# Hybrid diffusion block: the input projections of layer 0 start on rows that are scaled but not shifted, and layer 1 starts three such projections instead of five

## The chip, the cores and the metric

One NeuronCore of a Trainium2 chip runs the whole program. The metric is the device time of one execution in microseconds (us), the median of several runs; lower is better. Engines are named as in the profile: PE (TensorE matmuls) and PEld (its weight loads), DVE (VectorE), ACT (ScalarE), POOL (GpSimd), SP (SyncE, which issues the DMAs).

## The reference, cut to what matters

Two layers over 384 columns: 128 context tokens (stream 0) and 256 latent tokens (stream 1), each with its own modulation vector, model width 1024. What matters here is the head of each layer:

```
mod = silu(cond) @ w_ada + b_ada              # one vector per stream
sh1, sc1, g1, sh2, sc2, g2 = split(mod, 6)
h   = rmsnorm(x, norm1_g) * (1 + sc1) + sh1
parts = split(h @ w_in, ...)                  # inputs of three mixers and of their gates
```

The mixers (windowed attention A, latent attention B, a gated delta rule C with a 3-tap convolution in front), their gated sum, an output projection and a squared-ReLU MLP follow.

## The kernel before, in words

Data lie transposed, features on the 128 partitions and the T = 384 tokens along the free axis, so the model width is 8 blocks `k`. Every float32 product is made of float32r halves: `split` (L145 to L147) makes a high part on ACT (L146, `whi`) and the rest on DVE (L147, `wlo`), and `mm3` (L149 to L152) makes three matmuls per `k`. A *projection tile* is 128 outputs: 8 blocks, 24 matmuls, into one PSUM bank. Banks come from pools: `pg` (three banks, tag `g`), `po` (one, `o`), `pc` (two, `c`), `pf` (a pair, `f`, taken by `twin`). A tile framework fixes each engine's order of instructions beforehand from the order of the program and its priorities; every engine then runs its own list in order.

**Layer 0** has the function `lead` (L352 to L414), because its modulation has to be computed from `w_ada` first. It takes `w_ada` in three parts, `PARTS`: four blocks `k` of scale and shift together (eight DMAs of 512 KB), then two and two (sixteen DMAs of 256 KB). For each part, PE multiplies it with the condition (`c<-mraw,cs`, L155, 32 output columns, four matmuls per DMA), DVE transposes the result (L400), adds the bias (L402) and forms the gain `gp` (L404). `modulated` (L216 to L229) then makes the finished `h` of those blocks as `hh` and `hl`: DVE L223 (x times gain times the row factor `rb`), ACT L225 (plus shift, high part), DVE L226 (the rest). Four projection tiles, `w_small` (48 outputs: the decoupled key and the gates of mixer C) and three conv keys of mixer C, run along as far as `h` goes (`advance`). Their banks are two `g` and more; the first is read by ACT into `kab`, the others by the convolution `conv_silu` (ACT L648, DVE L651, L653, ACT L657, DVE L658).

**Layer 1** has its modulation early, but needs the row factor `rb`. So `scaled` (L231 to L244) makes `x` times gain without `rb`, with the shift in two extra columns T and T+1, and five projection tiles (L482 to L490) run on that: three `g` banks and the pair `f`. Meanwhile `modulated` makes the finished `h` for the rest. `normalised` (L546 to L555) later turns such a bank into the finished projection: DVE copies the shift's columns to `eb` (L550) and multiplies by `rb` (`rbs`, L551), ACT adds `eb` (L553).

After the head both layers transpose `kab` (L595), run the chain of the gates on DVE (`z`, `lp`, `gdec`, L597 to L638), and go on with the other tiles of `w_in` through `project` (one `g` bank each): keys and values of mixer A first (`kA`, with the rotation `rope` on DVE: L250 to L253).

Of the kernel before, what the change touches and what calls it, by code (L numbers as in the profile page):

```python
# [18 lines left out]
P = 128  # L19
# [8 lines left out]
B_SCALE = 96.0 ** -0.5  # L28
STREAMS = ((0, slice(0, 128)), (1, slice(128, 384)))

PARTS = ((4, 2), (2, 1), (2, 1))

ADV = (2, 1, 3, 1, 0, 1, 0, 1, 2, 1, 2, 3)

# [10 lines left out]
def trunk(ctx: ExitStack, tc: tile.TileContext, A, O):  # L45
# [4 lines left out]
    def mk(pool, shape, tag, dt=F32, bufs=None):  # L50
        count[0] += 1
        return pool.tile(list(shape), dt, name=f"{tag}_{count[0]}", tag=tag, bufs=bufs)
# [161 lines left out]
    def hidden():  # L214
        return mk(hp, [P, T + 2], "hh", F32R, bufs=KT), mk(hp, [P, T + 2], "hl", F32R, bufs=KT)

    def modulated(rb, gp, sh, sh0, ks=range(KT)):
        his, los = [], []
        for k in ks:
            t = mk(sp, [P, T], "tmp")  # L220
            hi, lo = hidden()
            for s, c in STREAMS:
                V.scalar_tensor_tensor(out=t[:, c], in0=x[k][:, c], scalar=gp[:, k, s:s + 1], in1=rb[:, c],  # L223
                                       op0=ALU.mult, op1=ALU.mult)
                S.activation(hi[:, c], t[:, c], AF.Identity, bias=sh[:, sh0 + k, s:s + 1], scale=1.0)  # L225
                V.scalar_tensor_tensor(out=lo[:, c], in0=t[:, c], scalar=sh[:, sh0 + k, s:s + 1],  # L226
                                       in1=hi[:, c].bitcast(F32), op0=ALU.add, op1=ALU.subtract)
            his.append(hi)
            los.append(lo)  # L229
        return his, los  # L230

    def scaled(gp, sh, sh0):

        his, los = [], []
        for k in range(KT):
            hi, lo = hidden()
            for s, c in STREAMS:
                S.activation(hi[:, c], x[k][:, c], AF.Copy, scale=gp[:, k, s:s + 1])
                V.scalar_tensor_tensor(out=lo[:, c], in0=x[k][:, c], scalar=gp[:, k, s:s + 1],  # L239
                                       in1=hi[:, c].bitcast(F32), op0=ALU.mult, op1=ALU.subtract)  # L240
            split(sh[:, sh0 + k, :], hi[:, T:], lo[:, T:])
            his.append(hi)
            los.append(lo)
        return his, los  # L244
# [105 lines left out]

    early = []

    def lead():
        es = ExitStack()
        lp = area(es, "lead", "right")
        pl = prm[0]
        rb = mk(lp, [P, T], "rb")
        S.copy(rb, rstd_rows(squares(x), 1.0 / DM))
        mod0 = mods[0, 0] = mk(sp, [P, 16, 2], "mod0")
        m0 = mod0.rearrange("p (s b) i -> p s b i", s=2)  # L360
        gp1 = mk(sp, [P, KT, 2], "gp1")
        srcs = [A["w_small"][0]] + [A["w_in"][0, 11 + i] for i in range(4)]
        tiles, at, hh, hl, pair = [], [], [], [], []

        def load():
            src = srcs.pop(0)
            n = src.shape[1]
            raw = mk(wp, [P, 1024], "raw", bufs=3)
            nc.sync.dma_start(raw[:, :n], src)
            hi, lo = mk(lp, [P, 1024], "lhi", F32R, bufs=5), mk(lp, [P, 1024], "llo", F32R, bufs=5)  # L370
            split(raw[:, :n], hi[:, :n], lo[:, :n])
            if len(tiles) == 3:
                pair[:] = twin()
            ps = mk(pg, [P, 512], "g") if len(tiles) < 3 else pair[len(tiles) - 3]
            tiles.append([w[:, :n].rearrange("p (k c) -> p k c", k=KT) for w in (hi, lo)])
            early.append(ps[:n // KT, :T])
            at.append(0)

        def advance(k1):
            for i, (wh, wl) in enumerate(tiles):  # L380
                for k in range(at[i], k1):
                    mm3(early[i], wh[:, k, :], wl[:, k, :], hh[k][:, :T], hl[k][:, :T], k == 0, k == KT - 1)
                at[i] = k1

        b0 = 0
        for nb, nw in PARTS:
            n, b1 = 2 * nb, b0 + nb
            for _ in range(nw):
                load()
            ps = bank()  # L390
            for k in range(KT):
                raw = mk(lp, [P, n * P], f"mraw{nb}", bufs=KT)
                nc.sync.dma_start(raw.rearrange("p (s c) -> p s c", s=2),
                                  A["w_ada"][0, k * P:(k + 1) * P, 0:2048].rearrange("p (s c) -> p s c", s=2)[:, :, b0 * P:b1 * P])
                rv = raw.rearrange("p (b g i) -> p g b i", g=4, i=32)
                for g in range(4):
                    mm(ps[32 * g:32 * g + 32, :32 * n].rearrange("p (b i) -> p b i", b=n), cs[:, k, :], rv[:, g],
                       start=k == 0, stop=k == KT - 1)
            tr = mk(sp, [P, 512], "diag", bufs=1)[:, :32 * n]
            V.transpose(out=tr, in_=ps[:, :32 * n])  # L400
            bias = pl[:, Q_ADA:Q_ADA + 16].rearrange("p (s b) -> p s b", s=2)[:, :, b0:b1].unsqueeze(3).to_broadcast([P, 2, nb, 2])
            V.tensor_tensor(out=m0[:, :, b0:b1, :], in0=tr.rearrange("p (s b i) -> p s b i", s=2, i=32)[:, :, :, 0:2], in1=bias,  # L402
                            op=ALU.add)
            V.scalar_tensor_tensor(out=gp1[:, b0:b1, :], in0=m0[:, 1, b0:b1, :], scalar=1.0,  # L404
                                   in1=pl[:, Q_N1 + b0:Q_N1 + b1].unsqueeze(2).to_broadcast([P, nb, 2]),
                                   op0=ALU.add, op1=ALU.mult)
            his, los = modulated(rb, gp1, mod0, 0, range(b0, b1))
            hh += his
            hl += los
            advance(b0)  # L410
            b0 = b1
        advance(KT)
        es.close()
        return hh, hl  # L414


    def attend(pool, q, k, vals, mask, scale, sink, oT):
# [52 lines left out]
    for l in range(DEPTH):  # L470
        pl = prm[l]
        phase(4 * l)
        if l == 0:
            xs = load_x(0, A["xT"])
            hh, hl = lead()
        else:
            rb = rstd_rows(squares(x), 1.0 / DM)
            mod0 = mods[l, 0]
            gp1 = gain(mod0, KT, l, Q_N1, "gp1")

            xh, xl = scaled(gp1, mod0, 0)
            pss = []  # L482
            banks = [mk(pg, [P, 512], "g") for _ in range(3)] + twin()
            for ps, w in zip(banks, weights([A["w_small"][l]] + [A["w_in"][l, 11 + i] for i in range(4)])):
                wh, wl = (t.rearrange("p (k c) -> p k c", k=KT) for t in w)
                M = wh.shape[2]
                ps = ps[:M, :T + 2]
                for k in range(KT):
                    mm3(ps, wh[:, k, :], wl[:, k, :], xh[k], xl[k], k == 0, k == KT - 1)
                pss.append(ps)  # L490
            hh, hl = modulated(rb, gp1, mod0, 0)
            rbs = mk(sp, [P, T], "sqacc", bufs=1)
            S.copy(rbs, rb)
            early += pss
# [51 lines left out]
        def normalised(t, ps):  # L546

            M = ps.shape[0]
            b = mk(sp, [P, 2], "eb")[:M]
            V.tensor_copy(b, ps[:, T:])  # L550
            V.tensor_tensor(out=t, in0=ps[:, :T], in1=rbs[:M], op=ALU.mult)  # L551
            for s, c in STREAMS:
                S.activation(t[:, c], t[:, c], AF.Identity, bias=b[:, s:s + 1], scale=1.0)  # L553
            return t

        ps, kab = early.pop(0), mk(sp, [48, T], "kab", bufs=1)
        if l == 0:
            S.copy(kab, ps)
        else:
            normalised(kab, ps)  # L560
        nc.sync.dma_start(O["krT"][l], kab[0:32, 0:128])
        if l == 0:
            nc.sync.dma_start(cst[:, C_M5:], A["const"][:, C_M5:])
# [14 lines left out]
        def g4():  # L578
            return mk(ccp, [P, 4, P], "g", bufs=22)
# [168 lines left out]


        keys, queries = (mk(ccp, [P, 4, T], name, bufs=1) for name in ("keys", "queries"))  # L750
        done = [conv_silu(ps if l == 0 else normalised(flat(g4())[:, :T], ps), 4 + i, keys[:, i, :]) for i, ps in enumerate(early)]
        n_done = len(done)
        early.clear()
        ws = win(11 + n_done, 12 - n_done)
# [632 lines left out]
```

## Time and profile before

| | |
|---|---|
| median of 3 runs | 1537.96 us (1535.86 to 1540.34) |
| the profiled execution's own time | 1539.57 us |
| its span in the trace | 1537.8 us |
| mean granted clock of TensorE | 0.992 |
| PE busy | 97% of the span |
| PEld, DVE, ACT busy | 89%, 65%, 50% |

The profile is of one execution. Span and own time differ by 1.8 us that lie outside the trace. "Idle before" is the time an engine had nothing to run ahead of an instruction, and the name behind it is what ended that.

### The profile page before, as it was taken

How to read it: one execution, taken by the hardware profiler on the slowest of the kernel's cores; microseconds unless marked ns; L12 is line 12 of the kernel's file. 1: busy time of each engine (PE TensorE's matmuls, PEld its weight loads, DVE VectorE, ACT ScalarE, POOL GpSimd, SP SyncE). 2: the span in 40 equal slices, each digit the busy share in tenths (PEclk: the TensorE clock that was granted, in tenths of full speed). 3: DMA queues.
4: the chain of work that ended last, by engine and by line, in shares of the span. 5: the costliest groups of instructions: out<-in, count | busy, mean ns of one | idle time of the engine just before them, and what ended most of it. 6: DMA issues, size and time to landing. Idle time of an engine off the chain costs nothing. (4 is left out here: it accounts for less than half of the span.)

```text
span 1537.8 us, 25236 instructions
## 1 busy us (share of the span) xinstructions
PE 1488.8 (97%) x9694; PEld 1369.7 (89%) x9694; DVE 995.1 (65%) x2163; ACT 769.8 (50%) x1527; POOL 22.4 (1%) x82
## 2 busy tenths in 40 slices
PE   5999999999999999999997999999999999999997
PEld 2898788987889999999997988889889999999997
DVE  4677895564437788888858679955644665553333
ACT  3466634355424666633326566443554456663222
POOL 0000200000000000000000002000000000000000
PEclk9999999999999999999998999999999999999999
DMA  9532131243588466687743331312324344443342
GB/s 316 165 108 84 55 97 56 84 134 111 197 294 265 133 201 192 197 252 240 242 135 99 96 85 56 102 62 88 103 75 137 124 123 124 124 124 125 122 128 78
DMA packets 80856, 212.82 MB, mean 138 GB/s; under 512 B 8800, under 2 KB 24544, under 8 KB 80608
## 3 DMA queue, kind: packets, MB, share of 16 engines
q1 hardware_dynamic: 80736, 211.21, 43.9%
q8 instruction: 76, 1.25, 0.3%
q14 instruction: 44, 0.36, 0.1%
HBM read 204.59 MB, written 4.75 MB: 136 GB/s over the span
## 5 line engine op out<-in xcount | busy, mean ns | idle before, releaser
L146 ACT CAST whi<-raw 128x1024 fp32r<-128x1024 f32 x268 | 280.8, 1048 | 491.7 <-PE g L151 440.5
L150 PE MATMUL g<-hh,whi 128*128 128x384 f32 (+1 forms) x1424 | 489.0, 345 | 8.9 <-DVE kab L551 8.2
L152 PE MATMUL g<-hh,wlo 128*128 128x384 f32 (+1 forms) x1424 | 488.4, 344 | 4.0 <-DVE wlo L147 3.9
L151 PE MATMUL g<-hl,whi 128*128 128x384 f32 (+1 forms) x1424 | 486.2, 342 | 0.0
L147 DVE TENSOR_TENSOR wlo<-raw,whi 128x1024 fp32r<-128x1024 f32 x268 | 326.1, 1217 | 170.3 <-PE g L152 136.0
L150 PEld LDWEIGHTS g<-hh,whi 128*128 128x128 f32 x1424 | 268.8, 189 | 20.5 <-issue 16.6
L152 PEld LDWEIGHTS g<-hh,wlo 128*128 128x128 f32 x1424 | 268.6, 189 | 13.0 <-DVE wlo L147 8.2
L151 PEld LDWEIGHTS g<-hl,whi 128*128 128x128 f32 x1424 | 268.7, 189 | 5.9 <-issue 2.6
L152 PE MATMUL g<-fh,wlo 128*128 128x384 f32 x512 | 172.9, 338 | 1.7 <-DVE wlo L147 1.7
L150 PE MATMUL g<-fh,whi 128*128 128x384 f32 x512 | 173.2, 338 | 0.0
L151 PE MATMUL g<-fl,whi 128*128 128x384 f32 x512 | 172.3, 337 | 0.0
L319 DVE SCALAR_TENSOR_TENSOR aacc<-araw,cs,aacc 128x512 f32<-128x512 f32 x168 | 117.2, 746 | 14.2 <-DMA araw<-in_w_ada_dram 12.2
L152 PEld LDWEIGHTS g<-fh,wlo 128*128 128x128 f32 x512 | 96.0, 188 | 3.2 <-DVE wlo L147 3.2
L150 PEld LDWEIGHTS g<-fh,whi 128*128 128x128 f32 x512 | 96.0, 188 | 1.6 <-issue 1.6
L151 PEld LDWEIGHTS g<-fl,whi 128*128 128x128 f32 x512 | 96.0, 188 | 0.0
L150 PE MATMUL g<-brh,whi 128*128 128x384 f32 x192 | 65.8, 343 | 1.6 <-ACT gate L529 1.2
L436 ACT ACTIVATE at_p<-at_p,at_nm 128x384 f32<-128x384 f32 (+1 forms) x96 | 51.7, 540 | 29.7 <-DVE at_nm L433 29.1
L151 PE MATMUL g<-brl,whi 128*128 128x384 f32 x192 | 65.9, 343 | 0.0
L152 PE MATMUL g<-brh,wlo 128*128 128x384 f32 x192 | 65.6, 342 | 0.0
L147 DVE TENSOR_TENSOR fl<-fa,fh 128x384 fp32r<-128x384 f32 x64 | 35.6, 556 | 38.8 <-ACT fh L146 38.8
L347 DVE SCALAR_TENSOR_TENSOR x<-g,mod,x 128x128 f32<-128x128 f32 x64 | 23.7, 412 | 51.0 <-PE g L152 47.6
L1231 ACT ACTIVATE fa<-fa,fb 128x128 f32<-128x128 f32 (+1 forms) x128 | 51.1, 446 | 0.7 <-DVE fa L1229 0.7
(333 smaller groups left out, 1887.0 us busy)
## 6 DMA issues: line engine op xcount, KB each, us to landing
raw<-in_w_ff_dram SPq DMA_DIRECT2D x128, 512.0 KB, 3.7
raw<-in_w_in_dram SPq DMA_DIRECT2D x102, 512.0 KB, 3.6
araw<-in_w_ada_dram SPq DMA_DIRECT2D x96, 256.0 KB, 3.5
raw<-in_w_branch_dram SPq DMA_DIRECT2D x24, 512.0 KB, 3.7
araw<-in_w_ada_dram SPq DMA_DIRECT2D x24, 512.0 KB, 6.7
raw<-in_w_out_dram SPq DMA_DIRECT2D x16, 512.0 KB, 3.6
mraw<-in_w_ada_dram SPq DMA_DIRECT2D x8, 512.0 KB, 8.8
mraw<-in_w_ada_dram SPq DMA_DIRECT2D x16, 256.0 KB, 6.5
```

What stands on the lines that cost most here:

```text
L146: S.copy(hi, src)
L147: V.tensor_tensor(out=lo, in0=src, in1=hi.bitcast(F32), op=ALU.subtract)
L150: PE.matmul(ps, lhsT=wh, rhs=rh, start=start, stop=False)
L151: PE.matmul(ps, lhsT=wh, rhs=rl, start=False, stop=False)
L152: PE.matmul(ps, lhsT=wl, rhs=rh, start=False, stop=stop)
L319: V.scalar_tensor_tensor(out=acc[:, s, :], in0=raw, scalar=cs[:, k, s:s + 1], in1=acc[:, s, :], op0=ALU.mult, op1=ALU.add)
L347: V.scalar_tensor_tensor(out=x[k][:, c], in0=ps[:, c], scalar=m[:, b0 + k, s:s + 1], in1=x[k][:, c], op0=ALU.mult, op1=ALU.add)
L436: S.activation(sm[:, :nk], sm[:, :nk], AF.Exp, bias=nm[:, u:u + 1], scale=-1.0, accum_out=den[:, u:u + 1])
L1231: S.activation(a[:, c], a[:, c], AF.Relu, bias=b[:, s:s + 1])
```

## The change

In layer 0 `w_ada` comes in four parts of eight 256 KB DMAs: scale of blocks 0 to 3, scale of 4 to 7, then shift 0 to 3, shift 4 to 7. Projection tiles are five (`w_small` and four conv keys; `LOADS` says ahead of which part each weight is loaded), in the pair `f`, `o` and two `g`. They run on `x` times gain (`lxh`, `lxl`), which needs neither `rb` nor the shift. The shift joins last as four columns T to T+3 of the same banks: per block a matmul of the high weights with the shift's high and low halves (4 columns) and one of the low weights with its high halves (2 columns), 80 in all (L155). The finished `h` for the rest is made from `lt` (gain times `rb` times x) as the shift comes. `normalised` now serves layer 0 too, with `eb` four columns wide. From the second part on, each part's matmuls begin with its last DMA. In layer 1 three projections run unnormalised instead of five, in the pair `f` and one `g`.

```diff
-PARTS = ((4, 2), (2, 1), (2, 1))
+LOADS = (2, 1, 2, 0)
...
     def lead():
...
+        banks = [*twin(), bank(po, "o"), mk(pg, [P, 512], "g"), mk(pg, [P, 512], "g")]
+        tiles, at, xh, xl = [], [], [], []
...
-                    mm3(early[i], wh[:, k, :], wl[:, k, :], hh[k][:, :T], hl[k][:, :T], k == 0, k == KT - 1)
+                    mm3(early[i][:, :T], wh[:, k, :], wl[:, k, :], xh[k], xl[k], k == 0, k == KT - 1)
...
+        for part, nw in enumerate(LOADS):
             for _ in range(nw):
                 load()
+            b0 = (8, 12, 0, 4)[part]
             ps = bank()
+            raws = []
             for k in range(KT):
+                raws.append(mk(lp, [P, 512], "mraw", bufs=12))
+                nc.sync.dma_start(raws[k], A["w_ada"][0, k * P:(k + 1) * P, b0 * P:(b0 + 4) * P])
...
+                first = block(KT - 1, 0, True, False)
+                with tc.issue_after(first.ins):
...
+            if part < 2:
...
+                for k in range(k0, k0 + 4):
+                    hi, lo = mk(lp, [P, T], "lxh", F32R, bufs=KT), mk(lp, [P, T], "lxl", F32R, bufs=KT)
+                    scaled_tile(k, gp1, hi, lo)
...
+                advance(k0 + 4)
...
+        sh = mk(lp, [P, KT, 4], "lsh", F32R)
+        split(mod0[:, 0:KT, :], sh[:, :, 0:2], sh[:, :, 2:4])
+        for ps, (wh, wl) in zip(early, tiles):
+            for k in range(KT):
+                mm(ps[:, T:], wh[:, k, :], sh[:, k, :], k == 0, False)
+                mm(ps[:, T:T + 2], wl[:, k, :], sh[:, k, 0:2], False, k == KT - 1)
+        hh, hl = [], []
+        for k in range(KT):
+            hi, lo = hidden()
+            for s, c in STREAMS:
+                if s == 1 and k % 2 == 1:
+                    V.tensor_scalar(out=hi[:, c], in0=ts[k][:, c], scalar1=mod0[:, k, s:s + 1], scalar2=None, op0=ALU.add)
+                else:
+                    S.activation(hi[:, c], ts[k][:, c], AF.Identity, bias=mod0[:, k, s:s + 1], scale=1.0)
+                V.scalar_tensor_tensor(out=lo[:, c], in0=ts[k][:, c], scalar=mod0[:, k, s:s + 1],
+                                       in1=hi[:, c].bitcast(F32), op0=ALU.add, op1=ALU.subtract)
...
-            banks = [mk(pg, [P, 512], "g") for _ in range(3)] + twin()
-            for ps, w in zip(banks, weights([A["w_small"][l]] + [A["w_in"][l, 11 + i] for i in range(4)])):
+            banks = twin() + [mk(pg, [P, 512], "g")]
+            for ps, w in zip(banks, weights([A["w_small"][l]] + [A["w_in"][l, 11 + i] for i in range(2)])):
...
         def normalised(t, ps):
 
             M = ps.shape[0]
-            b = mk(sp, [P, 2], "eb")[:M]
+            b = mk(sp, [P, 4], "eb")[:M, :ps.shape[1] - T]
             V.tensor_copy(b, ps[:, T:])
+            if ps.shape[1] - T == 4:
+                V.tensor_tensor(out=b[:, 0:2], in0=b[:, 0:2], in1=b[:, 2:4], op=ALU.add)
...
-        ps, kab = early.pop(0), mk(sp, [48, T], "kab", bufs=1)
-        if l == 0:
-            S.copy(kab, ps)
-        else:
-            normalised(kab, ps)
+        kab = normalised(mk(sp, [48, T], "kab", bufs=1), early.pop(0))
```

How it moves instructions, at three places (a row is the line, the operation, output and inputs with their numbers, the output's tile; "x3" is three alike).

PE at the end of layer 0's head, before: `f_392` is the fourth early tile, `g_653` the first tile of the rest (keys of mixer A).

```order
L150 MATMUL f_392<-hh_456,lhi_388 128x384
L151 MATMUL f_392<-hl_457,lhi_388 128x384
L152 MATMUL f_392<-hh_456,llo_389 128x384
L595 MATMUL c_547<-cst_83,kab_529 128x48 x3
L150 MATMUL g_653<-hh_237,whi_649 128x384
L151 MATMUL g_653<-hl_238,whi_649 128x384
```

The same place now: `g_172` is the fifth early tile, `g_906` the keys of mixer A.

```order
L155 MATMUL g_172<-lsh_605,lhi_449 128x4
L155 MATMUL g_172<-lsh_605,llo_450 128x2
L150 MATMUL g_906<-hh_712,whi_902 128x384
L151 MATMUL g_906<-hl_713,whi_902 128x384
L152 MATMUL g_906<-hh_712,wlo_903 128x384
```

Seven rows further on, `g_945` being the values of mixer A:

```order
L151 MATMUL g_906<-hl_731,whi_902 128x384
L152 MATMUL g_906<-hh_730,wlo_903 128x384
L635 MATMUL c_764<-cst_83,kab_741 128x48 x3
L150 MATMUL g_945<-hh_688,whi_941 128x384
L151 MATMUL g_945<-hl_689,whi_941 128x384
```

The 80 small matmuls stand in the middle of `g_906`, whose blocks 0 to 3 run ahead of them and whose blocks 4 to 7 behind; the transposes of `kab` come behind `g_906`.

DVE now, behind those matmuls: `kab`, `g_830`, `g_845`, `g_860` are the evictions of the early tiles, `wlo_986` the low half of a later weight, `rp_a` and `rp_b` the rotation of `g_906`, `z`, `beta`, `sa` the gates.

```order
L595 TENSOR_TENSOR kab_741<-f_169,sqacc_122 48x384
L592 COPY eb_831<-f_169 128x4
L147 TENSOR_TENSOR wlo_986<-raw_983,whi_985 128x1024
L594 TENSOR_TENSOR eb_831<-eb_831 128x2
L595 TENSOR_TENSOR g_830<-f_169,sqacc_122 128x384
L637 TENSOR_TENSOR z_768<-c_764,prm_6_90 128x24
L592 COPY eb_846<-o_170 128x4
L247 TENSOR_TENSOR rp_a_932<-g_906,cst_83 128x256
L640 TENSOR_SCALAR beta_770<-beta_770 128x24
L658 TENSOR_SCALAR z_768<-z_768 128x24
L594 TENSOR_TENSOR eb_846<-eb_846 128x2
L248 STREAM_SHUFFLE rp_b_933<-g_906 128x256
```

Before, DVE had no `kab`, `eb` or eviction by `rb` there in layer 0; now the cast `wlo_986` stands between the eviction of `kab` and everything that the gates and the rotation need.

PE at the head of layer 1, before: `f_8303` is the fifth unnormalised tile, `g_8693` the first on the finished `h`.

```order
L152 MATMUL f_8303<-hh_8292,wlo_8427 128x386
L150 MATMUL g_8693<-hh_8455,whi_8689 128x384
L595 MATMUL c_8555<-cst_83,kab_8541 128x48
L151 MATMUL g_8693<-hl_8456,whi_8689 128x384
L595 MATMUL c_8555<-cst_83,kab_8541 128x48 x2
```

The same place now: `g_8515` is the third unnormalised tile and ends 45 rows ahead of these; `g_8856` is the second of the two tiles that follow it on the finished `h`, `g_8900` the next.

```order
L150 MATMUL g_8856<-hh_8670,whi_8852 128x384
L151 MATMUL g_8856<-hl_8671,whi_8852 128x384
L152 MATMUL g_8856<-hh_8670,wlo_8853 128x384
L635 MATMUL c_8707<-cst_83,kab_8693 128x48 x3
L727 MATMUL f_8884<-cst_83,tmp_8881 128x128 x3
L150 MATMUL g_8900<-hh_8607,whi_8896 128x384
```

Two tiles on the finished `h`, `g_8817` and `g_8856`, take turns block by block in place of the fourth and fifth unnormalised tile, and the transposes of `kab` and of the values (L727) come behind them, ahead of the next tile.

## Rows read from the trace of the kernel before

**Rows 1.** The page's part 1: busy time, share of the span, instructions of each engine.
```profile
PE 1488.8 (97%) x9694; PEld 1369.7 (89%) x9694; DVE 995.1 (65%) x2163; ACT 769.8 (50%) x1527; POOL 22.4 (1%) x82
```

**Rows 2.** PE's waits: engine, line, what for: us in total, times, longest.
```profile
PE g L150 <- DVE kab L551: 8.2, 1, 8.2
```

**Rows 3.** Stretches of PE: from:to us, width, busy (instructions), granted clock, DMA share, GB/s.
```profile
26.00:27.00 1.00, 0.83 (x16) 0.60 1.09 347
33.00:34.00 1.00, 1.00 (x16) 0.98 1.10 344
227.00:228.00 1.00, 1.00 (x20) 0.80 0.06 16
818.00:819.00 1.00, 0.00 (x0) 0.55 1.11 332
828.00:829.00 1.00, 1.00 (x7) 0.83 0.00 0
```

**Rows 4.** Timeline of PE, layer 0: start, us, operation, count [idle before <-releaser].
```profile
12.32 1.44 PE L155 MATMUL c<-cst,sqacc 128*128 128x1 f32 x6 [12.32 <-DVE sqacc L211]
22.55 0.64 PE L155 MATMUL c<-mraw,cs 128*32 128x256 f32 x8 [0.73 <-DMA mraw<-in_w_ada_dram]
23.90 0.64 PE L155 MATMUL c<-mraw,cs 128*32 128x256 f32 x8 [0.71 <-DMA mraw<-in_w_ada_dram]
27.33 1.20 PE L150 MATMUL g<-hh,lhi 128*48 128x384 f32 x3
38.97 0.86 PE L155 MATMUL c<-mraw,cs 128*32 128x128 f32 x24
53.01 0.38 PE L595 MATMUL c<-cst,kab 48*128 48x48 f32 x3
53.60 0.33 PE L151 MATMUL g<-hl,whi 128*128 128x384 f32 x1
61.62 0.34 PE L152 MATMUL g<-hh,wlo 128*128 128x384 f32 x1
62.91 1.48 PE L155 MATMUL c<-cst,g 128*128 128x1 f32 x12
226.34 0.33 PE L155 MATMUL f<-blk,g 64*64 64x64 f32 x4 [1.67 <-DVE blk L944]
227.27 1.52 PE L155 MATMUL f<-blk,g 64*64 64x64 f32 x28
```

**Rows 5.** Timeline of DVE, layer 0.
```profile
24.61 0.45 DVE L400 STREAM_TRANSPOSE diag<-c 128x256 f32<-128x256 f32 x1 [7.93 <-PE c L155]
60.19 0.18 DVE L616 SCALAR_TENSOR_TENSOR lp<-lp,s 128x24 f32<-128x24 f32 x1
60.28 0.34 DVE L653 SCALAR_TENSOR_TENSOR g<-f,cw,g 128x127 f32<-128x127 f32 x1
60.63 0.48 DVE L651 SCALAR_TENSOR_TENSOR g<-f,cw,g 128x255 f32<-128x255 f32 x1
62.04 0.44 DVE L251 STREAM_SHUFFLE rp_b<-g 128x256 f32<-128x256 f32 x1
62.45 1.22 DVE L147 TENSOR_TENSOR wlo<-raw,whi 128x1024 fp32r<-128x1024 f32 x1
```

**Rows 6.** Timelines of PE, DVE and ACT, layer 1.
```profile
812.82 0.34 PE L152 MATMUL f<-hh,wlo 128*128 128x386 f32 x1
821.32 0.66 PE L150 MATMUL g<-hh,whi 128*128 128x384 f32 x1 [8.16 <-DVE kab L551]
...
820.63 0.54 DVE L551 TENSOR_TENSOR kab<-g,sqacc 48x384 f32<-48x384 f32 x1
...
804.60 1.05 ACT L146 CAST whi<-raw 128x1024 fp32r<-128x1024 f32 x1 [3.23 <-PE g L151]
809.74 1.49 ACT L225 ACTIVATE hh<-tmp,mod 128x128 fp32r<-128x128 f32 x4
821.21 0.80 ACT L553 ACTIVATE kab<-kab,eb 48x128 f32<-48x128 f32 x2 [0.65 <-DVE kab L551]
```

More of the change, by code (lines that the diff above doesn't have):

```diff
@@ L236, in scaled @@
             hi, lo = hidden()
[L237 to L240, printed above, removed]
+            scaled_tile(k, gp, hi, lo)
             split(sh[:, sh0 + k, :], hi[:, T:], lo[:, T:])
@@ L351, in trunk, with scaled_tile @@
     early = []
+    def scaled_tile(k, gp, hi, lo):
+        for s, c in STREAMS:
+            S.activation(hi[:, c], x[k][:, c], AF.Copy, scale=gp[:, k, s:s + 1])
+            V.scalar_tensor_tensor(out=lo[:, c], in0=x[k][:, c], scalar=gp[:, k, s:s + 1],
+                                   in1=hi[:, c].bitcast(F32), op0=ALU.mult, op1=ALU.subtract)
     def lead():
@@ L356, in lead @@
         pl = prm[0]
-        rb = mk(lp, [P, T], "rb")
+        rb = mk(sp, [P, T], "sqacc", bufs=1)
         S.copy(rb, rstd_rows(squares(x), 1.0 / DM))
         mod0 = mods[0, 0] = mk(sp, [P, 16, 2], "mod0")
-        m0 = mod0.rearrange("p (s b) i -> p s b i", s=2)
         gp1 = mk(sp, [P, KT, 2], "gp1")
         srcs = [A["w_small"][0]] + [A["w_in"][0, 11 + i] for i in range(4)]
-        tiles, at, hh, hl, pair = [], [], [], [], []
+        banks = [*twin(), bank(po, "o"), mk(pg, [P, 512], "g"), mk(pg, [P, 512], "g")]
+        tiles, at, xh, xl = [], [], [], []
         def load():
@@ L371, in load @@
             split(raw[:, :n], hi[:, :n], lo[:, :n])
-            if len(tiles) == 3:
-                pair[:] = twin()
-            ps = mk(pg, [P, 512], "g") if len(tiles) < 3 else pair[len(tiles) - 3]
+            early.append(banks[len(tiles)][:n // KT, :T + 4])
             tiles.append([w[:, :n].rearrange("p (k c) -> p k c", k=KT) for w in (hi, lo)])
-            early.append(ps[:n // KT, :T])
             at.append(0)
@@ L381, in advance @@
                 for k in range(at[i], k1):
-                    mm3(early[i], wh[:, k, :], wl[:, k, :], hh[k][:, :T], hl[k][:, :T], k == 0, k == KT - 1)
+                    mm3(early[i][:, :T], wh[:, k, :], wl[:, k, :], xh[k], xl[k], k == 0, k == KT - 1)
                 at[i] = k1
-        b0 = 0
-        for nb, nw in PARTS:
-            n, b1 = 2 * nb, b0 + nb
+        for part, nw in enumerate(LOADS):
             for _ in range(nw):
                 load()
+            b0 = (8, 12, 0, 4)[part]
@@ L390, in lead @@
             ps = bank()
+            raws = []
             for k in range(KT):
[L392 to L412, printed above, removed]
+                raws.append(mk(lp, [P, 512], "mraw", bufs=12))
+                nc.sync.dma_start(raws[k], A["w_ada"][0, k * P:(k + 1) * P, b0 * P:(b0 + 4) * P])
+            def block(k, g, start, stop):
+                rv = raws[k].rearrange("p (b g i) -> p g b i", g=4, i=32)
+                return mm(ps[32 * g:32 * g + 32, :128].rearrange("p (b i) -> p b i", b=4), cs[:, k, :], rv[:, g],
+                          start=start, stop=stop)
@@ new lines, in lead @@
+            if part == 0:
+                for k in range(KT):
+                    for g in range(4):
+                        block(k, g, k == 0, k == KT - 1)
+            else:
+                first = block(KT - 1, 0, True, False)
+                with tc.issue_after(first.ins):
+                    for g in range(1, 4):
+                        block(KT - 1, g, True, False)
+                    for k in range(KT - 1):
+                        for g in range(4):
+                            block(k, g, False, k == KT - 2)
@@ new lines, in lead @@
+            tr = mk(sp, [P, 512], "diag", bufs=1)[:, :128]
+            V.transpose(out=tr, in_=ps[:, :128])
+            V.tensor_tensor(out=mod0[:, b0:b0 + 4, :], in0=tr.rearrange("p (b i) -> p b i", i=32)[:, :, 0:2],
+                            in1=pl[:, Q_ADA + b0:Q_ADA + b0 + 4].unsqueeze(2).to_broadcast([P, 4, 2]), op=ALU.add)
+            if part < 2:
+                k0 = 4 * part
+                V.scalar_tensor_tensor(out=gp1[:, k0:k0 + 4, :], in0=mod0[:, b0:b0 + 4, :], scalar=1.0,
+                                       in1=pl[:, Q_N1 + k0:Q_N1 + k0 + 4].unsqueeze(2).to_broadcast([P, 4, 2]),
+                                       op0=ALU.add, op1=ALU.mult)
+                for k in range(k0, k0 + 4):
+                    hi, lo = mk(lp, [P, T], "lxh", F32R, bufs=KT), mk(lp, [P, T], "lxl", F32R, bufs=KT)
+                    scaled_tile(k, gp1, hi, lo)
+                    xh.append(hi)
+                    xl.append(lo)
+                advance(k0 + 4)
@@ new lines, in lead @@
+            if part == 1:
+                ts = [mk(lp, [P, T], "lt", bufs=KT) for _ in range(KT)]
+                for k in range(KT):
+                    for s, c in STREAMS:
+                        V.scalar_tensor_tensor(out=ts[k][:, c], in0=x[k][:, c], scalar=gp1[:, k, s:s + 1], in1=rb[:, c],
+                                               op0=ALU.mult, op1=ALU.mult)
+            if part == 2:
+                advance(KT)
+        sh = mk(lp, [P, KT, 4], "lsh", F32R)
+        split(mod0[:, 0:KT, :], sh[:, :, 0:2], sh[:, :, 2:4])
@@ new lines, in lead @@
+        for ps, (wh, wl) in zip(early, tiles):
+            for k in range(KT):
+                mm(ps[:, T:], wh[:, k, :], sh[:, k, :], k == 0, False)
+                mm(ps[:, T:T + 2], wl[:, k, :], sh[:, k, 0:2], False, k == KT - 1)
+        hh, hl = [], []
+        for k in range(KT):
+            hi, lo = hidden()
+            for s, c in STREAMS:
+                if s == 1 and k % 2 == 1:
+                    V.tensor_scalar(out=hi[:, c], in0=ts[k][:, c], scalar1=mod0[:, k, s:s + 1], scalar2=None, op0=ALU.add)
+                else:
+                    S.activation(hi[:, c], ts[k][:, c], AF.Identity, bias=mod0[:, k, s:s + 1], scale=1.0)
+                V.scalar_tensor_tensor(out=lo[:, c], in0=ts[k][:, c], scalar=mod0[:, k, s:s + 1],
+                                       in1=hi[:, c].bitcast(F32), op0=ALU.add, op1=ALU.subtract)
+            hh.append(hi)
+            hl.append(lo)
@@ L413, in lead @@
         es.close()
-        return hh, hl
+        return hh, hl, rb
     def attend(pool, q, k, vals, mask, scale, sink, oT):
@@ L474, in trunk @@
             xs = load_x(0, A["xT"])
-            hh, hl = lead()
+            hh, hl, rbs = lead()
         else:
@@ L750, in trunk @@
         keys, queries = (mk(ccp, [P, 4, T], name, bufs=1) for name in ("keys", "queries"))
-        done = [conv_silu(ps if l == 0 else normalised(flat(g4())[:, :T], ps), 4 + i, keys[:, i, :]) for i, ps in enumerate(early)]
+        done = [conv_silu(normalised(flat(g4())[:, :T], ps), 4 + i, keys[:, i, :]) for i, ps in enumerate(early)]
         n_done = len(done)
```

## The prediction

> **What bounds the kernel now.** I read the page first, then PE's waits, then its stretches with the clock, then the timelines of the two heads. PE is busy for 1488.8 of 1537.8 us [rows 1], so only what it waits, or runs at half clock, can be won. Of its waits one is large and single: 8.2 us for DVE's eviction of `kab` at the head of layer 1 [rows 2]; in layer 0 PE stands between bursts of `mraw`, the DMAs of `w_ada` [rows 4]. Each place has a tail. TensorE's granted clock has two levels, 2.4 and 1.2 GHz (1.00 and 0.50 in the rows, a slice in which it changes shows a value between). It falls at about 26.2 and comes back at about 33.0; it falls at 818.1 and comes back at 828.3 [rows 3]. The change works at these two places.
>
> **Layer 0: the start.** PE multiplies `w_ada` as its blocks land, one of 512 KB every 23.90 - 22.55 = 1.35 us; the last burst ends at 24.54 and the first matmul on `h` comes at 27.33 [rows 4]. The first part is half as large now, which takes 4 x 1.35 = 5.4 us off: it ends at about 19.1. The transpose (0.45 us before [rows 5], half the width now), the bias and the gain follow; then ACT makes the high half straight from `x`, where DVE's L223 stood ahead of it. I put the first projection matmul 1.6 us after the last burst, at 20.7, so 6.6 us earlier.
>
> **Layer 0: to the end of the sixth tile.** Before, four early tiles and two of the rest are done at 61.8 [rows 4]; now five early tiles and `g_906`. Work from 20.7 on:
> - 6 x 24 = 144 matmuls. In steady state 46 of them take 61.62 - 53.60 = 8.02 us [rows 4], 0.174 each: 25.1 us.
> - The other three parts of `w_ada`, 96 matmuls with 32 output columns; 24 took 0.86 us [rows 4], 0.036 each: 3.5 us. Each part's matmuls start with its last DMA, so PE isn't split up by arrivals; by the pace of the DMAs (0.7 us for 256 KB) part 2 of four is there at 25.5 and part 3 at 34, ahead of PE. The last four DMAs of part 4 wait until PE has read part 3 (12 buffers), and the weights of `g_906` queue behind them on SP: they land at about 44.5, and with a cast of 1.05 on ACT [rows 6] and one of 1.22 on DVE [rows 5] the low half is ready at 46.7 to 47, where PE wants it at 46.4. I take 0.8 us of wait.
> - The first 12 matmuls are paced by DVE's low halves (0.95 us over their own time).
> - The shift: 80 matmuls of 4 or 2 columns, nothing like them in number before. The nearest row is 12 one-column matmuls on 128x128 weights, 1.48 us, 0.123 each [rows 4]: the weight load sets the pace, not the columns. 64 have 128 output columns; 16 have 48, for which I take 0.05, between the 0.036 of 32 columns and 0.123. 64 x 0.119 (one end's latency taken off) + 0.8 = 8.4 us. They can't start before DVE has split the shift, behind the cast `wlo_942`; that is about when `g_906`'s first half ends, so I add nothing.
>
> Sum: 20.7 + 25.1 + 3.5 + 0.8 + 0.95 + 8.4 = 59.5, against 61.8: 2.3 us won. The 8.4 us of the shift eat what the earlier start and the vanished half clock give.
>
> How cheap could the shift be? The trace's quickest small matmuls are 28 with 64x64 weights in 1.52 us, 0.054 each, part of them at half clock [rows 4]: 80 of these are 4.3 us, 4.1 less than my sum. At the other end stands the cold row: six one-column matmuls in 1.44 us, 0.24 each [rows 4], twice my price. I take 0.119, since load and array size are the same there. The Trainium skill, page TensorE: Matmul & The Clock Gate, section Back-to-back issue gap, gives 1 to 64 columns a floor of about 25 ns where no load stands between them; by that alone 80 would be an estimated 2.0 us, and the row with loads in it speaks against it.
>
> **Layer 0: what is late next.** Before, `kab` and the convolutions had been under way while the two tiles ran, and the transposes of `kab` came at 53.01 [rows 4]. Now DVE, after evicting `kab`, stands in the cast `wlo_986` until `g_906` has ended and its buffer is free, and everything behind waits. `g_945` needs `g_906`'s bank, which DVE's shuffle frees. From the end of `g_906`: the cast 1.22, an eviction 0.54 [rows 6], six small operations of 0.18, rotation 0.42 (read as the shuffle's 0.44) and shuffle 0.44 [rows 5], less some 0.08 of overlap at each of nine seams: 3.0 us idle. ACT's `kab` path (cast 1.05, two halves 0.80 [rows 6]) runs beside and ends sooner. The next tile, `g_989`, waits for the eviction `g_860`, 24 DVE operations after the shuffle: eleven of 0.34 to 0.54 (4.9 together) and thirteen small ones of 0.18 [rows 5, 6], less 24 seams: 5.3 us; the tile in front takes 4.2, so 1.1 more are idle. Together 4.1, less the 0.2 us of `kab`'s transposes that are counted in the 61.8 before. Layer 0: -2.3 + 4.1 - 0.2 = 1.6, rounded up to **+2.0 us** for the seams.
>
> **Layer 1.** Before, five unnormalised tiles end at 813.16, PE idles to 821.32, and the clock is half until 828.3 [rows 3, 6]: 7.0 us at half speed cost 3.5. Now the fourth and fifth tile run on the finished `h`, in two banks that are free. DVE can start that `h` when the third tile takes the buffers over, at about 802, and needs some 10.7 us for it (before, from ACT's first `hh` at 809.74 to the eviction of `kab` at 820.63, 10.9, with two weight casts between [rows 6]), so both end at about 813.5, level with before. What remains is `kab`: ACT has a cast of 1.05 in front (it waits for the first of the two tiles), then the two halves 0.80 [rows 6], so the transposes come at 814.6. The values' transposes, still in front of the next tile, wait for ACT's copy behind the evictions, to 816.7. The tile starts at 817.0: 4.3 us earlier than 821.3, and at full clock, since the fall came at 818.1, 4.9 us after the last matmul [rows 3, 6]. **-7.8 us**. Taking both tiles out of the five costs nothing by itself: 48 matmuls stay 48, two columns less.
>
> **Sum.** 2.0 - 7.8 = -5.8 us on the profiled execution's own 1539.57: 1533.8. That execution is 1.6 above the median of the runs, so **1532.2** for the median. About 0.3% (4.6 us) is what a measurement of this kernel can tell from no change.
>
> **Rivals.**
> - *The clock falls in the shift (no change).* 8.4 us with 4 moving columns per load may not keep it up. For: it fell at 26.2 after bursts that used a quarter of the columns. Against: there PE had stood idle from 24.54 to 26.06, and at 226.3 for 1.67 us before the fall at 227.2 [rows 3, 4]; in the shift it is never idle. Falling 5 us in, the last 3.4 us double (+3.4), `g_906`'s twelve matmuls cost 2.1 more, half of the next tile another 2.1; the wait of 1.1 before `g_989` vanishes. +6.5: 1538.7.
> - *Slower: the clock falls early in the shift.* Same place, but after 3.1 us, as at 226.3 (idle from 224.7, fall at 227.2 to 228.0): 5.3 us double (+5.3), +2.1, the whole next tile at half speed because the return took 7 us after work resumed at 821.3 (+4.2), -1.1: +10.5, 1542.7. It decides if the fall comes within some 3.5 us of the first small matmul; from there on the layer-1 gain is more than spent.
> - *The small matmuls are cheap.* With loads hidden behind one another at 0.054, 4.1 less: 1528.1. By the Trainium skill's floor in the sentence above it would be an estimated 6.4 less. For: PEld is busy beside PE for most of the span [rows 1]; against: the row of 12.
> - *The layer-1 bank gain doesn't come.* If `kab` or the values wait until about 821 behind ACT's evictions, only the fall of the clock is saved or not even that: +2 to -1.5, 1536 to 1540. Against it stands that nothing in that chain waits for the last block of `h`.
>
> **The numbers.** Chances: the sum as it stands 0.45, clock falling late 0.2, early 0.13, cheap 0.12, no gain in layer 1 0.1. My own case spreads by about 3 us (the two walks), so some 0.3 of its 0.45 is under 1533.3, with nearly all of the cheap case and a little of the rest: faster 0.45. Slower needs over 1542.6: the early fall and the tails of the late one and of the last case, 0.17. Same: 0.38. The range from 1527.5 to 1542.5 takes in the cheap case and all but the worst of the early fall. The forecast case alone: 1529 to 1536.
>
> **What would show it.** Right: first projection matmul at 20 to 21.5; 80 matmuls L155 with `lsh` over 8 to 9 us, clock 1.00; then about 3 us of PE idle ended by DVE's shuffle or the eviction before `g_945`, and about 1 before `g_989`; the wait of 8.2 for `kab` in layer 1 gone, a tile starting near 817, clock 1.00 throughout 813 to 830. Wrong: a slice at 0.50 between 48 and 75 (rivals one and two); the small matmuls under 6 us (rival three); a PE wait over 6 us at the head of layer 1 (rival four); or a difference after 70 and before 790, where I expect none.

## The result, and the profile after

The changed kernel takes 1546.94 us (four runs, 1546.21 to 1547.97) against 1536.91 us before (four runs): ratio 1.0062, 95% interval 1.0046 to 1.0077. It is slower by about 10 us; the forecast was 1532.2 us, in a range from 1527.5 to 1542.5. Layer 1 gained about what was forecast, layer 0 lost far more.

PE in the head of layer 0, the changed kernel's timeline (columns as in [rows 4]):

```profile
20.72 0.37 PE L150 MATMUL f<-lxh,lhi 128*48 128x384 f32 x1 [1.68 <-ACT lxh L352]
24.82 0.45 PE L150 MATMUL f<-lxh,lhi 128*128 128x384 f32 x1
...
27.98 1.95 PE L155 MATMUL c<-mraw,cs 128*32 128x128 f32 x64
29.86 0.44 PE L152 MATMUL o<-lxh,llo 128*128 128x384 f32 x1
...
52.28 0.17 PE L155 MATMUL f<-lsh,lhi 128*48 128x4 f32 x1
52.99 0.25 PE L155 MATMUL f<-lsh,lhi 128*128 128x4 f32 x1
...
55.67 0.26 PE L155 MATMUL o<-lsh,lhi 128*128 128x4 f32 x1
55.79 0.35 PE L155 MATMUL o<-lsh,llo 128*128 128x2 f32 x1
...
63.90 0.35 PE L155 MATMUL g<-lsh,llo 128*128 128x2 f32 x1
64.11 0.67 PE L150 MATMUL g<-hh,whi 128*128 128x384 f32 x1
...
69.46 0.84 PE L635 MATMUL c<-cst,kab 48*128 48x48 f32 x3 [1.17 <-ACT kab L597]
71.67 0.66 PE L150 MATMUL g<-hh,whi 128*128 128x384 f32 x1 [1.36 <-DVE sa L648]
```

The first projection matmul comes at 20.72 where 27.33 stood [rows 4]. The shift's 80 matmuls run from 52.28 to 64.11, 11.8 us without a gap. Up to 55.79 one with 48 outputs takes (52.99 - 52.28) / 16 = 0.044 us and one with 128 outputs (55.67 - 52.99) / 24 = 0.112; from there each takes (64.11 - 55.79) / 39 = 0.213. The same kernel's stretches show why (columns as in [rows 3]):

```profile
22.00:23.00 1.00, 1.00 (x5) 0.50 1.04 383
25.00:26.00 1.00, 1.00 (x8) 0.97 1.04 416
55.00:56.00 1.00, 1.00 (x10) 0.89 0.99 300
56.00:57.00 1.00, 1.00 (x6) 0.50 1.01 319
75.00:76.00 1.00, 1.00 (x5) 0.50 0.00 0
76.00:77.00 1.00, 1.00 (x7) 0.87 0.00 0
830.00:831.00 1.00, 1.00 (x6) 0.80 0.53 86
```

The clock fell to 1.2 GHz 3.5 us after the first small matmul, with PE busy all the time, and came back at about 76.3, 20.5 us later. It had also been down from 21.6 to 25.1. These are the times of one execution: in the profile of the same layer 0 under "Layer 0 alone" below the clock fell 4.5 us after the first small matmul (58.3 behind 53.86), was down for 10.2 us, and fell once more at 72.0 for 3.4. What DVE did meanwhile (its timeline):

```profile
55.96 0.14 DVE L592 COPY eb<-f 128x4 f32<-128x4 f32 x1
68.39 1.22 DVE L147 TENSOR_TENSOR wlo<-raw,whi 128x1024 fp32r<-128x1024 f32 x1 [12.29 <-issue]
71.08 0.44 DVE L248 STREAM_SHUFFLE rp_b<-g 128x256 f32<-128x256 f32 x1
```

That is the cast `wlo_986`, as the order said: DVE stands for 12.29 us until `g_906` has ended at 68.1, and PE then starts `g_945` at 71.67, after the shuffle (the profile names the small operation right behind it, `sa`).

In layer 1 PE's timeline answers to [rows 6]:

```profile
826.79 0.72 PE L635 MATMUL c<-cst,kab 48*128 48x48 f32 x3 [0.61 <-ACT kab L597]
829.27 0.55 PE L727 MATMUL f<-cst,tmp 128*128 128x128 f32 x3 [1.76 <-ACT tmp L723]
829.57 0.42 PE L150 MATMUL g<-hh,whi 128*128 128x384 f32 x1
```

The wait of 8.2 us [rows 2] is gone; the fifth tile ends at 826.2 and the next starts at 829.57. But the clock falls here too, at 830.6 for 3.4 us, behind the two waits that remain (0.61 and 1.76).

Where the time went shows at PE's first matmul of the MLP (`fh`) in each layer, before:

```profile
649.14 0.45 PE L150 MATMUL g<-fh,whi 128*128 128x384 f32 x1
1390.11 0.34 PE L150 MATMUL g<-fh,whi 128*128 128x384 f32 x1
```

and after:

```profile
664.50 0.45 PE L150 MATMUL g<-fh,whi 128*128 128x384 f32 x1
1396.77 0.34 PE L150 MATMUL g<-fh,whi 128*128 128x384 f32 x1
```

Layer 0's head and mixers cost 15.4. From `fh` to `fh` it is 740.97 before and 732.27 after, 8.7 less. The two profiled executions are 6.6 us apart (1539.57 and 1546.21), the medians 10.0.

### The profile page after: what moved, and what is told of

It is laid out like the page before. It is cut to its first block, busy times and chain, and to the rows that moved or that the text cites. A ratio compares the mean times of both kernels' runs of the same rounds, so it can differ in the third digit from the quotient of the medians.

```text
span 1544.4 us, 25606 instructions
## 1 busy us (share of the span) xinstructions
PE 1501.1 (97%) x9838; PEld 1391.2 (90%) x9838; DVE 1004.9 (65%) x2196; ACT 774.3 (50%) x1545; POOL 22.3 (1%) x82
## 4 chain that ended last, share of the span: by engine, by line
PE 85%; DVE 10%; ACT 2%; issue 1%; DMA 1%; SPq 0%; DVEq 0%; ACTq 0%
PE g L150 22%; PE g L152 22%; PE g L151 21%; PE c L155 6%; PE f L155 3%; PE o L155 2%; PE g L155 2%; DVE wlo L147 2%; PE f L497 2%; DVE blk L911 1%; DVE h L909 1%; DVE hl L353 1%; PE c L150 1%; PE c L152 1%; PE c L151 1%
```

## The experiments

Each ran with the kernel before beside it; ratios are to that, with their 95% interval.

**Layer 1 alone.** The kernel before with the change's two lines for layer 1:

```diff
-            banks = [mk(pg, [P, 512], "g") for _ in range(3)] + twin()
-            for ps, w in zip(banks, weights([A["w_small"][l]] + [A["w_in"][l, 11 + i] for i in range(4)])):
+            banks = twin() + [mk(pg, [P, 512], "g")]
+            for ps, w in zip(banks, weights([A["w_small"][l]] + [A["w_in"][l, 11 + i] for i in range(2)])):
```

> Layer 0 as before the change, layer 1 with three unnormalised projections. Theory A (layer 1 wins by itself, the whole loss is in layer 0): the 8.2 us wait for kab is gone, clock 1.00 from 785 to 830; 8 to 9 us under the kernel before, some 1528.5. Theory B (layer 1's gain in the changed kernel is only the clock having fallen elsewhere): within 3 us of the kernel before, 1534 to 1537.

Measured: 1532.34 us, ratio 0.9967 (0.9953 to 0.9981), 5 us faster. From `fh` to `fh` its profile shows 732.06, 8.9 less than before. Around there the clock does not hold as theory A had it: it dips at 819.3 for 3.4 us, behind the two waits that remained:

```profile
815.44 0.72 PE L595 MATMUL c<-cst,kab 48*128 48x48 f32 x3 [0.61 <-ACT kab L553]
817.92 0.55 PE L687 MATMUL f<-cst,tmp 128*128 128x128 f32 x3 [1.76 <-ACT tmp L683]
```

Theory A by the wait that went, though the median lies between the two theories' numbers. That it shows 5 and not 9 agrees with what else the profile has: 2.5 us more in layer 0, in code that is the same as before, where the clock was down at 187.8 for 3.4 us and at 228.8 for 6.8 (before, only at 227.6 for 3.4), and 0.9 more behind the last `fh`. The other executions were not traced.

**Layer 0 alone.** The changed kernel with those two lines turned back.

> Layer 0 as changed, layer 1 with five unnormalised projections as before. Theory A: the sum of the parts, 15 us over the kernel before, some 1552, with the 8.2 us wait for kab in layer 1 back. Theory B: under 1549.

Measured: 1554.18 us, ratio 1.0117 (1.0088 to 1.0146). PE waits 8.2 us for `kab` in layer 1 again. Theory A: the two parts add up (+16.5 and -5.4 against +10.0), and the whole loss is in layer 0. Its first `fh` is at 663.85, 14.7 later than before. From `fh` to `fh` its layer 1, the one before, takes 738.41, so the 8.7 of layer 1 is 6.1 against this profile.

**The shift in wide matmuls.** Zeros behind the shift's columns:

```diff
+        wide = []
+        sh = mk(lp, [P, KT, P], "lsh", F32R)
+        sh2 = mk(lp, [P, KT, P], "lsh2", F32R)
+        for t in (sh, sh2):
+            V.tensor_copy(t.rearrange("p k c -> p (k c)"), zeros.to_broadcast([P, KT * P]))
...
+            wide.append(banks[len(tiles)][:n // KT, T:T + P])
...
+        S.copy(sh2[:, :, 0:2], mod0[:, 0:KT, :])
-        for ps, (wh, wl) in zip(early, tiles):
+        for ps, (wh, wl) in zip(wide, tiles):
             for k in range(KT):
-                mm(ps[:, T:], wh[:, k, :], sh[:, k, :], k == 0, False)
-                mm(ps[:, T:T + 2], wl[:, k, :], sh[:, k, 0:2], False, k == KT - 1)
+                mm(ps, wh[:, k, :], sh[:, k, :], k == 0, False)
+                mm(ps, wl[:, k, :], sh2[:, k, :], False, k == KT - 1)
```

> The changed kernel with the 80 shift matmuls widened by zeros to 128 moving columns each; same 80 weight loads, result unchanged. Theory C (few moving columns let the clock fall): the clock stays at 1.00 through the shift, a matmul still takes 0.111 us at 128 outputs, the shift lasts 7.8 us in place of 11.8, and the time falls by about 8 us (4.0 in the shift, 1.9 in the tile that holds it, 2.1 in the next), to 1539. Theory D (the clock falls because PE waits for DVE and ACT around there): the clock falls all the same and the time stays at 1545 to 1547.

Measured: 1541.61 us, ratio 1.0023 (1.0012 to 1.0034), 5.3 under the changed kernel. The shift ran from 53.17 to 61.36, 8.2 us, at full clock; what came behind is another loss:

```profile
55.00:60.00 5.00, 5.00 (x47) 1.00 0.47 144
60.00:65.00 5.00, 4.05 (x28) 1.00 0.35 99
65.00:70.00 5.00, 0.40 (x1) 0.73 0.36 118
70.00:75.00 5.00, 5.00 (x23) 0.59 0.00 0
```

In these slices of 5 us the clock holds to 65. PE had begun a wait before that:

```profile
69.60 0.66 PE L150 MATMUL g<-hh,whi 128*128 128x384 f32 x1 [5.55 <-DVE gdec L667]
```

The framework ordered DVE and ACT anew (most of the gates' chain now runs ahead of the rotation), and the clock falls in that idle, at 67.3 for 6.8 us. Theory C for the shift; the new wait is more than the 2.6 us that are missing to its number.

**Ten of the 80 shift matmuls.** Only block 0's two matmuls for each tile; the kernel leaves out the shift of the other blocks.

> The changed kernel with 10 of the 80 shift matmuls; leaves out blocks 1 to 7 of the shift in the five early tiles of layer 0. Theory C: 70 x 0.111 less some 48-output ones, about 7 us of weight loads gone, and with a shift of 1 us no fall of the clock, another 8: 1532. Theory D: the loads go, the fall stays with the stall behind the first tile: 1539 to 1540.

Measured: 1534.79 us, ratio 0.9984 (0.9971 to 0.9998), 12 under the changed kernel, between the two theories: no fall in the shift, one at 58.0 for 6.8 us in the waits behind `g_906`, which are there as in the changed kernel (1.3 for `kab`, 1.4 for DVE). So once the shift no longer brings the clock down, it fell in these waits.

**Four early tiles, three forms of the shift.** One tile less leaves two `g` banks for the tiles that follow:

```diff
-LOADS = (2, 1, 2, 0)
+LOADS = (2, 1, 1, 0)
...
-        banks = [*twin(), bank(po, "o"), mk(pg, [P, 512], "g"), mk(pg, [P, 512], "g")]
+        banks = [*twin(), bank(po, "o"), mk(pg, [P, 512], "g")]
```

> The changed kernel with four early tiles in layer 0 instead of five, so that two banks of the pool g are free behind the head. Theory S (the wait behind the first tile of the rest is for its bank, which DVE and ACT free late): the 3.6 us of waits and transposes between that tile and the next shrink to the transposes alone and the later 1 us of waits goes; the shift has 64 matmuls, still at half clock at the end: 1540 to 1542. Theory O (the wait comes from the order on DVE and ACT whatever bank is free): 1545 or more.

> Four early tiles and the widened shift matmuls (128 moving columns, zeros behind the four). Theories C and S together: no fall of the clock between 27 and 75 us, shift of 64 matmuls in about 6.1 us, no wait over 1 us behind the first tile: 1532 to 1534. Theory O: a wait of 3 to 6 us stays behind the first or second tile, and the clock falls in it: 1537 to 1540.

The third form swaps the operands for all tiles but `w_small`:

```diff
+        for i, (wh, wl) in enumerate(tiles[1:]):
+            c = slice(i * P, (i + 1) * P)
+            for k in range(KT):
+                mm(st[0:4, c], sh[:, k, :], wh[:, k, :], k == 0, False)
+                mm(st[0:2, c], sh[:, k, 0:2], wl[:, k, :], False, k == KT - 1)
+        sT = mk(lp, [4, nt * P], "lst")
+        S.copy(sT, st[0:4, :nt * P])
+        for i, ps in enumerate(early[1:]):
+            mm(ps[:, T:], sT[:, i * P:(i + 1) * P], ident[0:4, 0:4])
```

> Four early tiles, and for the three conv keys the shift is the stationary operand (4 or 2 columns) and the weights move (128 columns); the sums come as 4 rows and are turned by three small matmuls. Theory C and the price by the longer of load and stream: 16 x 0.045 + 48 x 0.056 = 3.4 us in place of 6.1, clock at 1.00: 1529 to 1531. If a matmul with a 4-column load still costs 0.111: as e6, 1532 to 1534.

> The changed kernel, five early tiles, with the swapped operands for its four conv keys. Shift 0.7 + 64 x 0.056 = 4.3 us at full clock in place of 11.8, and the half clock behind it gone, but the wait for the bank as in the changed kernel: 1535 to 1537 by theories C and S; under 1533 if the bank is no limit (theory O).

Measured: narrow 1546.62 (ratio 1.0062), wide 1539.88 (1.0014; 0.9998 to 1.0029), swapped 1542.07 (1.0029), swapped with five tiles 1543.23 (1.0034). The last three scatter over 11 to 12 us from run to run. The narrow and the wide one have theory O's numbers, the swapped ones neither theory's. With four tiles none has O's mechanism: the waits behind the first tile did go with the free banks, in the narrow version PE waits 0.6 us between 53 and 75 (theory S). With five tiles, and so no free bank, PE waits 6.9 us for DVE's eviction of an early tile (L606) up to 69.32, and the clock falls in that wait, at 67.4 for 6.8 us: the bank is a limit, as theory S has it, at a higher price than forecast. In the versions with four tiles a wait had come in front, which no theory had (PE's waits, swapped version, 20 to 90 us):

```profile
PE c L155 <- DMA mraw<-in_w_ada_dram: 2.5, 1, 2.5
PE f L150 <- ACT lxh L352: 1.7, 1, 1.7
PE c L155 <- DVE gpiece L181: 1.7, 1, 1.7
PE g L152 <- DVE wlo L147: 0.6, 1, 0.6
PE g L150 <- ACT whi L146: 0.6, 1, 0.6
```

With 24 matmuls less in front, PE reaches the fourth part of `w_ada` before its last four DMAs have landed; they wait for buffers that PE frees with the third part, and the weights of the next tile queue behind them. In the changed kernel the fifth tile had covered this.

**More buffers.**

```diff
-                raws.append(mk(lp, [P, 512], "mraw", bufs=12))
+                raws.append(mk(lp, [P, 512], "mraw", bufs=16))
```

> The version with four early tiles and swapped operands, with 16 buffers for w_ada instead of 12 (and four instead of five for the early weights, as many as are used). Theory Q (in it the last four DMAs wait for buffers and the weights of the first tile queue behind them on SP: waits of 2.5, 0.6 and 0.6 us): these go, 3 to 4 us less, 1538 to 1539. Rival (the DMAs come at their rate whatever buffers there are): within 1 us of the version with 12, 1541 to 1543.

Measured: 1531.79 us, ratio 0.9962 (0.9948 to 0.9976), 10 us under the version with 12. Theory Q, and more than its number: the waits of 2.5, 0.6 and 0.6 are 0.2 together, that of 1.7 for `gpiece` is gone with the fall of the clock behind it. A new wait of 1.1 us, for DVE's split of the shift, stands just ahead of the shift. Profile against profile this is 3.7 (1536.65 and 1532.95); the rest lies in the scatter of the version with 12, whose profiled run was its fastest, and was not traced. Its shift:

```profile
48.72 0.18 PE L155 MATMUL f<-lsh,llo 128*48 128x2 f32 x1
48.77 0.22 PE L155 MATMUL c<-lhi,lsh 128*4 128x128 f32 x1
48.82 0.22 PE L155 MATMUL c<-llo,lsh 128*2 128x128 f32 x1
...
51.58 0.23 PE L155 MATMUL c<-llo,lsh 128*2 128x128 f32 x1
```

48 swapped matmuls take (51.58 - 48.77) / 47 = 0.060 us each, all 64 take 3.6.

**The clock's price, by itself.** On top of that version, the narrow and the wide form again, now without the wait for `w_ada`; the wait of 1.1 us ahead of the shift is in both.

> As the version with four tiles, 16 buffers and swapped operands (1531.8 us), but with the shift as in the changed kernel: 64 matmuls of 4 or 2 columns on the weights as stationary operand. Theory C: 16 x 0.045 + 48 x 0.111 = 6.0 us at full clock in place of 3.6, and the clock falls within 3 to 7 us of the first of them and stays half for 10 to 20 us: the doubled rest and the tiles behind cost 6 to 9 us; 1540 to 1543. If the fall in the changed kernel needed the stall behind the tile too: 1534.

> The same with the 64 matmuls widened to 128 columns by zeros: the same weight loads. Theory C: no fall, 2.4 us more than the swapped version, 1534 to 1535; the difference to the narrow version is the price of the half clock alone, 6 to 8 us. If loads and not columns decide: as the narrow version.

Measured: narrow 1540.17 us, ratio 1.0021 (1.0007 to 1.0035); wide 1534.45 us, ratio 0.9984 (0.9974 to 0.9995). Both times as theory C had them, their difference a little under its 6 to 8. The onset was earlier than its 3 to 7 us: the narrow one's clock fell 1.9 us after the first small matmul and was down for 13.7. The wide one's clock held through the shift and fell at 67.4, 13 us behind its end, for 3.4. The narrow one's stretches:

```profile
50.00:55.00 5.00, 5.00 (x25) 0.50 0.00 2
55.00:60.00 5.00, 5.00 (x20) 0.50 0.24 70
```

and the wide one's:

```profile
50.00:55.00 5.00, 4.86 (x43) 1.00 0.29 77
55.00:60.00 5.00, 4.87 (x28) 1.00 0.98 293
```

Same 64 weight loads: 5.7 us for the half clock, by the medians and by the first `fh` of the two profiles (658.61 and 652.86). From wide to swapped the shift itself is 2.7 us shorter (6.35 and 3.62); the medians say 2.7 too, but come from two series of runs, and each against its own kernel before gives 3.8.

**Two or four projections in layer 1**, with layer 0 as before the change.

> Layer 0 as before the change, two unnormalised projections in layer 1 (the pair f), three g banks free. Theory E (DVE can start the finished h a tile earlier, so the evictions and kab come earlier and PE's waits of 0.6 and 1.8 us there go, with the fall of the clock behind them): 1528.5 to 1530. Rival (kab and the values wait for casts on ACT that wait for PE's tiles, whatever DVE does): 1532 to 1533, as with three.

> Layer 0 as before, four unnormalised projections in layer 1 (the pair f and two g), one g bank free. DVE starts the finished h a tile later than with three, at about 806.5, and needs 10.7 us, while PE has one tile to 809 and then one paced by h: an idle of some 4 us at 813 and no fall of the clock or a short one. By theory A 1533 to 1535, between the version with three and the kernel before. If the gain with three came from the free banks alone and not from DVE's start: 1532.

Measured: two 1535.9 us (0.9984; 0.9973 to 0.9996), four 1538.35 us (0.9992; 0.9979 to 1.0005); three had 1532.3. Two is a miss for both theories: PE, with the finished `h` needed a tile sooner, waits for it in pieces (1.2 us for ACT's `hh`, 1.0 for `hl`), then 1.3 for `kab`, and the clock is half from 808.1 to 814.9. Four is some 3.4 us above its estimate of 1533 to 1535, with a wait of 1.4 for an eviction and one of 1.3 for `kab` added to those for `h` and a fall at 822.3; its profile is of the slowest of its ten executions, with 2.4 us more in layer 0 than before.

## Why the prediction was wrong

**Layer 1** stands in the main. Forecast -7.8, from `fh` to `fh` -8.7 (-6.1 against the profile of layer 0 alone), and the stations hold: between the fifth tile's end and the next tile's start 3.4 us (forecast 813.5 to 817.0), with the waits for `kab` and the values as ordered. What failed there is the clock of 1.00 throughout: it fell behind these waits, at 830.6 in the changed kernel and at 819.3 in the run of layer 1 alone, for 3.4 us each, in place of 10.2 before. That runs gain 5 from it alone is told above.

**Layer 0: the step that failed** is the choice between the forecast and its second rival: that the clock would hold through the shift because PE is never idle in it. It fell 3.5 us in, near the 3.1 of that rival, and stayed down for 20.5 us. The reason given against it (each fall seen before had PE idle for 1.5 us or more) was true of the rows and no ground: the bursts ahead of the fall at 26.2 had also used few output columns (128*32 in [rows 4], not 128*128), and no row showed a long run of matmuls with few moving columns. (Of the falls in its list the middle one is at 227.6 by [rows 3], not 227.2.) The runs that differ in the moving columns on the same loads settle it: with 4 or 2 columns the clock fell during the shift in all four profiles (the changed kernel, layer 0 alone, four tiles with 12 and with 16 buffers), with 128 columns in none of three. The Trainium skill, page TensorE: Matmul & The Clock Gate, Part 1: The HAM clock gate, says that the clock follows how busy PE has been and warns of gaps; here PE was busy by the profile's count in every slice and the clock fell, so that warning is narrower than what the trace shows.

The walk to the end of the sixth tile, forecast 59.5, measured 68.1, term by term:
- Start at 20.7: right (20.72). But the clock was half from 21.6 to 25.1, so the first 12 matmuls took 4.1 instead of 3.05: +1.05.
- The three other parts of `w_ada`: mis-sized. The row "x24" counts two records for each f32 matmul, as the changed kernel's "x64" for 32 of them shows; one part takes (29.86 - 27.98) = 1.9 us, not 1.2: +2.1. (The rows of 6 and of 12 one-column matmuls count so too.)
- The wait of 0.8 for the weight behind the last part's DMAs: there is none in the trace, its low half is ready at 50.4, where PE wants it. About as much went, 0.1 us each, into the changes between bursts and tiles, which the sum had at nothing: 0.
- The shift at full clock: 16 x 0.044 + 64 x 0.112 = 7.9 against 8.4: -0.5, so the price by the row of 12, one weight load for each record, held. The Trainium skill, page TensorE: Matmul & The Clock Gate, section LDWEIGHTS, has a load take its columns / 1.2 in ns, 0.107 and 0.040 us here, and the trace agrees to 0.005 us at full clock. The 25 ns of its section Back-to-back issue gap, cited with the cheap rival, did not apply with a load in front of each.
- The shift as it ran: 11.8, +3.9 by the half clock, and +1.9 on `g_906`'s twelve matmuls behind it (4.0 in place of 2.1).

Sum +8.5 of the 8.6.

**What is late next** was right: 3.0 us forecast between `g_906` and `g_945`, 3.6 measured with `kab`'s transposes, at half clock, in it, by the same cast and shuffle; then half a tile at half clock (+2.15, as the first rival had it; the second had the whole tile, +4.2). The 1.1 before `g_989` did not come, as both rivals said; 1.1 us came inside `g_989`, in front of the values' transposes.

So the second rival, 1542.7, was right in mechanism and place. How near its onset came is in part luck: over the four profiles with the narrow shift it was 1.6 to 4.5 us, and the clock stayed down for 10.2 to 20.5. It is 4.2 us short of the median of 1546.94. Of these 1.6 are what the forecast took off because the profiled execution before was above its median, and 0.7 that the changed one is below its own; so the profiled execution is 1.9 over (1546.21, where the rival's terms on 1539.57 make 1544.3): layer 0 cost 15.4, not 12.5, and layer 1 gave 8.7, not 7.8. In layer 0 the sizes above (+2.1 and +1.05) are partly made up by the half tile that the rival had too much. The changed profile also shows half clock at 325.4, 960.3 and 1001.3 for 3.4 us each, where the one before has a single such fall at 227.6; what these cost has not been taken apart. The rivals on cheap matmuls and on a lost layer-1 gain fell.

Why the start that was won didn't pay at all: PE came 6.6 us earlier and spent 3.4 us less at half clock there (21.6 to 25.1 in place of 26.2 to 33.0), worth 1.7 more; against these 8.3 stand, even at full clock, 7.9 us of weight loads that did not exist before, and behind them the waits of 3.6. Of the versions of the change's layer 0 the swapped shift, four tiles and 16 buffers together bring it level: in the 1531.79 version the first `fh` in layer 0 is at 651.85, where the kernel with layer 1 alone has 651.68, and the profile before, with the same layer 0 as that one, 649.14.

**What beats both kernels:** layer 1's part alone (1532.34) and the repaired whole (1531.79) are each about 0.35% faster than before, and can't be told apart; the first is two changed lines.

## What to carry to other kernels

Price a run of small matmuls by its weight loads, and then ask what it does to TensorE's clock: a busy PE that streamed 4 or 2 columns per load lost it here, as an idle one did elsewhere in these traces, and the price (5.7 us) came close to that of the loads themselves (6.35 in the same pair of runs). Where one operand is narrow, make it the stationary one, so that the load is short and the long side streams. And when work moves to the front of a program, look for what had been covered by it: here a weight cast queued on DVE and a PSUM bank, together behind a stop of 3.6 us, and four DMA buffers, worth 3.7 from profile to profile, once their cover was gone.

## What was not expected of the hardware

- Widening a matmul from 4 to 128 moving columns on the same 128x128 weights cost nothing by itself, 0.112 us each in both forms (on the 48-column weights 0.059 in place of 0.044), and the clock held at 1.00 through the shift, 5.7 us to the good.
- A matmul with a 4-column load and 128 moving columns took 0.060 us, half of the 0.112 that 128-column loads with 4 moving columns take.
- After the fall at 55.8 the clock did not come back while PE streamed full tiles from 64.11 to 68.1, nor in the 3.6 us behind them, but only 4.6 us into the next tile, at 76.3. In the run of layer 0 alone it came back at 68.6, at the end of the same tile.
- The profile counts a plain float32 matmul as two records, a float32r one as one: 32 matmuls of `w_ada` read x64, the 80 of the shift 80.
